# Low parts of weights by an adding DMA, and six more seven-product groups, in a hybrid decoder layer

## The chip, the cores and the metric

The kernel runs on one core of a Trainium2 chip. The metric is the device time of one launch in microseconds (us); lower is better. Times of several runs are given by their median.

## The reference

One decoder layer on a sequence of 256 tokens with 2048 features, all in float32: a norm and one combined projection, a state-space (SSD) head group and an attention head group, an output projection with a norm and residual, then a squared-ReLU MLP with a norm and residual. Cut to what matters here:

```python
def reference(x, ...):
    mix = hybrid_mixer(rmsnorm(h, norm_mix_pre), w_in, ..., w_out)   # w_in 2048 x 12320, w_out 4096 x 2048
    h = h + rmsnorm(mix, norm_mix_post)
    ff = squared_relu_mlp(rmsnorm(h, norm_mlp_pre), w_up, w_down)    # w_up 2048 x 8192, w_down 8192 x 2048
    return h + rmsnorm(ff, norm_mlp_post)

def squared_relu_mlp(u, w_up, w_down):
    hdn = jax.nn.relu(jnp.einsum('bsd,df->bsf', u, w_up))
    return jnp.einsum('bsf,fd->bsd', hdn * hdn, w_down)
```

Nearly all the work is the four matrix products of 256 tokens with these weights, each weight being used once.

## The kernel before, in words

**Split operands.** Products run on TensorE in a reduced float32 format. Every operand is therefore split into two parts: `hi`, a rounded copy, and `lo`, the rest (source minus hi). A product of two operands is three matmuls: hi by hi, hi by lo, lo by hi. ScalarE makes `hi` (L139, in `split`), VectorE makes `lo` by a subtraction (L140).

**Weight tiles.** A weight tile is 128 partitions by 2 row blocks by 512 columns (512 KB). `fetch` loads it from HBM on SP's queue into one of four `raw` buffers (L149; in w_out and in the last w_down the room `uc` serves as further raw buffers, through `fetch_next`). `parts` takes one of five `hi` and one of five `lo` buffers in turn. So tile number i can be split only when TensorE has done with tile number i - 5.

**Ordinary tiles.** `row_tile` (L262 to L264) multiplies one tile with one of the two token blocks: 2 row blocks by 3 matmuls, 128x512 each. An ordinary tile is thus 12 matmuls, and a row step k of a pair of column blocks (two tiles) 24.

**Seven-product groups.** `seven` replaces the pair of tiles of a row step by a fast scheme for 2 by 2 blocks, with seven block products instead of eight, so 21 matmuls (L344 to L346) instead of 24. In return VectorE makes four sums of weights (`add_in_line`, L225) and the sums, e, a and b, and a short t, are all split: four hi and four lo buffers a group. The sums of the activations of a row step are made once by `sums_of_acts` (L302 to L305 and a split) and kept, while their room lasts, for all column blocks. At the end of a pair of column blocks `combine_new` or `combine_onto` adds up what the groups left in further accumulators.

**Units.** `unit` does a pair of column blocks: a list of row steps (`order_of(steps, sevens)`), each ordinary or a group, then the last steps one column block at a time. The values of w_in, the whole of w_out, w_up and w_down run as units. w_up and w_down run in two halves of 4096 features (`hf`). The room for the sums is taken from tensors idle at that time: `in_place_of_u` (w_out and the last w_down: six sums), `in_place_of_h` (w_up three, the first w_down five).

**Order.** Loads, splits and additions of the units run ahead of TensorE: `high_priority` puts them first, and `in_line` keeps the splits and additions of VectorE and ScalarE in the order in which they are written. The scheduling layer fixes the order on each engine when the kernel is built; the engines then wait for one another by semaphores. `mw` holds the mixer's output and later that of w_down; `h` is kept in HBM meanwhile.

Of the kernel before, what the change touches and what calls it, by code (L numbers as in the profile page):

```python
# [10 lines left out]
F32 = mybir.dt.float32  # L11
F32R = mybir.dt.float32r
BF16 = mybir.dt.bfloat16
AF = mybir.ActivationFunctionType
ALU = mybir.AluOpType

P = 128
S = 256
D = 2048
NT = S // P  # L20
# [19 lines left out]
KB = 2  # L40
# [10 lines left out]
FIRST = 3  # L51
UP_SEVENS = (2, 4, 5)
V_SEVENS = (1, 3, 5, 6)


def constants():
# [18 lines left out]
def hymba_layer(ctx: ExitStack, tc: tile.TileContext, x, norm_mix_pre, w_in, conv_w, conv_b, dt_bias, a_log,  # L75
                d_skip, ssm_norm_w, w_out, norm_mix_post, norm_mlp_pre, w_up, w_down, norm_mlp_post,
                consts, out):
    nc = tc.nc
    w_in, w_out, w_up, w_down = w_in[0], w_out[0], w_up[0], w_down[0]
# [44 lines left out]
    def bank():  # L124
        return pacc.tile([P, NB], F32, name="acc")
# [10 lines left out]
    def split(hi, lo, src, scale=None):  # L136

        if scale is None:
            return (nc.scalar.activation(hi, src, AF.Copy),  # L139
                    nc.vector.tensor_tensor(lo, src, hi.bitcast(F32), op=ALU.subtract))  # L140
        return (nc.scalar.activation(hi, src, AF.Copy, scale=scale),  # L141
                nc.vector.scalar_tensor_tensor(lo, src, scale, hi.bitcast(F32), op0=ALU.mult, op1=ALU.subtract))

    def fetch(src, k0, c0, step=KB, into=None):

        raw = wp.tile([P, KB, NB], F32, name="raw", bufs=RAWS) if into is None else into
        for j in range(0, KB, step):
            rs = slice((k0 + j) * P, (k0 + j + step) * P)
            nc.sync.dma_start(raw[:, j:j + step], src[rs, c0:c0 + NB].rearrange("(k p) n -> p k n", p=P))  # L149
        return raw  # L150
# [13 lines left out]
    room = {}  # L164
# [6 lines left out]
        room["acts"] = part  # L171
        sums_of.clear()

    def in_place_of_h(acts):

        a = hp.tile([P, 3 * KB, 2, S], F32R, name="ha")
        room["sums"] = [a[:, k] for k in range(3 * KB)]
        if acts is part:
            b = hp.tile([P, KB, 2, S], F32R, name="hb")
            room["sums"] += [b[:, k] for k in range(KB)]  # L180
            room["sums"] += [hp.tile([P, 2, S], F32R, name="wpost", bufs=2) for _ in range(2)]
        else:
            b = hp.tile([P, NT, NB], F32, name="hb")
            room["shared"] = [[b[:, t] for t in range(NT)],
                              [hp.tile([P, NB], F32, name="wpost", bufs=2) for _ in range(NT)]]
        room["raw"] = None
        room["acts"] = acts
        sums_of.clear()
# [10 lines left out]
    def parts():  # L199
        return [wp.tile([P, KB, NB], F32R, name=n, bufs=BUFS) for n in ("hi", "lo")]  # L200
# [8 lines left out]
    line = {}  # L209

    @contextmanager
    def in_line():

        with ExitStack() as order:
            for last in line.values():
                order.enter_context(tc.issue_after(last.ins))
            yield

    def split_in_line(hi, lo, raw):
        with in_line():  # L220
            line["act"], line["dve"] = split(hi, lo, raw)

    def add_in_line(dst, a, b):
        with in_line():
            line["dve"] = nc.vector.tensor_tensor(dst, a, b, op=ALU.add)  # L225

    def weights(src, k0, c0, fetch=fetch):

        with tc.high_priority(offset=AHEAD):
            raw = fetch(src, k0, c0)  # L230
            hi, lo = parts()
            if fetch is fetch_next:
                split_in_line(hi, lo, raw)
                return hi, lo
            line.clear()
            with ExitStack() as order:
                while behind:
                    order.enter_context(tc.issue_after(behind.pop().ins))
                split(hi, lo, raw)
        return hi, lo  # L240
# [11 lines left out]
    def drain():  # L252
        while waiting:
            pump()
# [38 lines left out]
    def sums_of_acts(k):  # L293

        if k in sums_of:
            return sums_of[k]
        places = room["sums"][2 * len(sums_of):][:2]
        h_, l_, r = room["acts"](k * KB)
        with tc.high_priority(offset=AHEAD):
            a, c = (tmp().rearrange("p (i s) -> p i s", s=P) for _ in range(2))  # L300
            ah_, al_ = (v[:, r:r + KB].bitcast(F32).rearrange("p j (t s) -> p j t s", t=NT) for v in (h_, l_))
            nc.vector.tensor_tensor(a.rearrange("p (j t) s -> p j t s", t=NT), ah_, al_, op=ALU.add)  # L302
            nc.vector.tensor_tensor(c[:, 0:2], a[:, 0::3], a[:, 1:2].to_broadcast([P, 2, P]), op=ALU.subtract)
            nc.vector.tensor_tensor(c[:, 2], a[:, 0], c[:, 1], op=ALU.add)
            nc.vector.tensor_tensor(c[:, 3], a[:, 2], c[:, 2], op=ALU.subtract)  # L305
            ch, cl = (v.rearrange("p b (t s) -> p (b t) s", t=NT) for v in places)
            split(ch, cl, c)
        sums_of[k] = ch, cl
        return ch, cl
# [49 lines left out]
    def order_of(ks, by_seven):  # L359
        return [(k, k in by_seven) for k in ks]  # L360

    def unit(src, n, order, last, acc, more, combine, lag=0, at_end=(None, None), first=True, ending=None):


        cols = (n * NB, (n + 1) * NB)
        sevens = [k for k, by_seven in order if by_seven]
        for i, (k, by_seven) in enumerate(order):
            if i + 1 < len(order) and order[i + 1][1]:
                sums_of_acts(order[i + 1][0])
            if by_seven:  # L370
                if k == sevens[0]:
                    drain()
                seven(src, *cols, k, acc, more, k == sevens[0], k == sevens[-1])
            else:
                for b in range(2):
                    row_tiles(src, cols[b], [k], acc[b::2], room["acts"], first and i == 0, False,
                              fetch=fetch_next)
            if k == sevens[-1]:
                combine(more)
        for b in range(2):  # L380
            if b and ending:
                ended.append(ending(cols[b], last, acc))
            else:
                row_tiles(src, cols[b], last, acc[b::2], room["acts"], False, True, lag if b else 0, at_end[b],
                          fetch=fetch if b else fetch_next)
# [423 lines left out]
    def in_place_of_last_heads():  # L809
# [4 lines left out]
        yield  # L814
        for k in V_SEVENS:
            sums_of_acts(k)
            yield

    def two_values(vb):
# [8 lines left out]
        def end(b):  # L828
            def at_end(t, a):
# [5 lines left out]

        unit(w_in[:, COL_V:], vb, order_of(range(7), V_SEVENS), (7,), acc, more,
             lambda x: combine_new([[v[:, t] for t in range(NT)] for v in values], x), 0, (end(0), end(1)))
# [240 lines left out]
    acc = [bank() for _ in range(2 * NT)]  # L1078
    early = 5
# [7 lines left out]
    hp = ctx.enter_context(tc.tile_pool(name="hp", bufs=1, reuse_waits="tile"))  # L1087
# [11 lines left out]
    mw = hp.tile([P, NT, D], F32, name="mw")  # L1099
# [10 lines left out]
    more = [psmall(), bank(), psmall(), bank()]  # L1110

    def whole(n):
        def at_end(t, a):
# [1 line left out]
                mixed(n, t, a)  # L1115
        return at_end

    unit(w_out, 0, order_of(range(early, 14), (6, 9, 12)), (14, 15), acc, more,
         lambda x: combine_new(in_mw(0), x), 0, (whole(0), whole(1)), first=False)
    for n in (2, 3):  # L1120
        load_wpost(norm_mix_post, n)
    acc, more = more, acc
# [71 lines left out]
    def out_of_place():  # L1194

        yield from copies(in_dram, of_h, 4)
        in_place_of_h(act_u)
        for k in UP_SEVENS:
            sums_of_acts(k)
            yield  # L1200

    def in_dram(t, cs):
        return h_d[:, t, cs]
# [24 lines left out]
    acc = gemm_features(w_up, NB, begun)  # L1228
# [6 lines left out]
    acc, more = [bank() for _ in range(2 * NT)], [psmall(), bank(), psmall(), bank()]  # L1235
    for hf in range(2):
        if hf:
            in_place_of_h(act_u)
        for fb in range(0 if hf else 2, 8, 2):
            unit(w_up[:, hf * 4096:], fb, order_of(range(6), UP_SEVENS), (6, 7), acc, more,  # L1240
                 lambda x: combine_new(room["shared"], x), 0, (up_end(fb, 0), up_end(fb + 1, 1)))
            acc, more = more, acc
        if hf == 0:
            in_place_of_h(part)
            unit(w_down, 0, order_of(range(14), (4, 6, 9, 11, 13)), (14, 15), acc, more,
                 lambda x: combine_new(in_mw(0), x), 0, (onto(0), onto(1)))
            unit(w_down, 2, order_of((0, 1, 4, 2, 6, 3, 9, 5, 11, 7, 13, 8), (4, 6, 9, 11, 13)), (10, 12, 14, 15), more, acc,
                 lambda x: combine_new(in_mw(2), x), 0, (onto(2), onto(3)))
# [13 lines left out]
    in_place_of_u()  # L1262
    for n in range(2):
        load_wpost(norm_mlp_post, n)
    unit(w_down[4096:], 0, order_of(range(14), (3, 6, 8, 11, 13)), (14, 15), acc, more,
         lambda x: combine_onto(0, x), 0, (complete(0), complete(1)))
    for n in (2, 3):
        load_wpost(norm_mlp_post, n)
# [26 lines left out]
```

## Time and profile before

| | before |
|---|---|
| time, median of 3 runs | 1474.52 us (1473.16 to 1475.57) |
| profiled execution, first to last instruction | 1471.1 us |
| matmul records, TensorE busy | 7216, 1461.2 us (99%) |
| VectorE busy | 1239.6 us (84%) |
| ScalarE busy | 861.1 us (59%) |
| GpSimd busy | 47.8 us (3%) |
| read from HBM | 281.78 MB, 194 GB/s over the span |

The profiled execution has its span from the first to the last instruction; its own time is not listed apart from the three above, which lie 2.1 to 4.5 us over the span. Matmuls are pipelined and overlap one another, so the duration of one is longer than the step from one to the next. In the rows of the profile PE is TensorE, PEld its weight loads, DVE VectorE, ACT ScalarE, POOL GpSimd, SP the queue that issues the loads; L140 is line 140 of the kernel, and `lo<-raw,hi` names what an instruction writes and reads.

### The profile page before, as it was taken

How to read it: one execution, taken by the hardware profiler on the slowest of the kernel's cores; microseconds unless marked ns; L12 is line 12 of the kernel's file. 1: busy time of each engine (PE TensorE's matmuls, PEld its weight loads, DVE VectorE, ACT ScalarE, POOL GpSimd, SP SyncE). 2: the span in 40 equal slices, each digit the busy share in tenths (PEclk: the TensorE clock that was granted, in tenths of full speed). 3: DMA queues.
4: the chain of work that ended last, by engine and by line, in shares of the span. 5: the costliest groups of instructions: out<-in, count | busy, mean ns of one | idle time of the engine just before them, and what ended most of it. 6: DMA issues, size and time to landing. Idle time of an engine off the chain costs nothing.

```text
span 1471.1 us, 20006 instructions
## 1 busy us (share of the span) xinstructions
PE 1461.2 (99%) x7216; PEld 1231.4 (84%) x7216; DVE 1239.6 (84%) x1849; ACT 861.1 (59%) x1188; POOL 47.8 (3%) x67
## 2 busy tenths in 40 slices
PE   9999999999999999999999999999999999999998
PEld 8888888888888888888888888888888888888886
DVE  6798797898497696588989989889887898989998
ACT  7475675465456565555557566655554666665553
POOL 0003100210000000000000000000000000000000
PEclk9999999999999999999999999999999999999999
DMA  7665566555657476566657566655665666576853
GB/s 272 208 205 182 179 184 194 174 172 167 177 168 207 122 208 192 191 229 210 204 177 237 165 194 201 210 175 191 213 223 174 201 201 205 172 235 202 273 200 114
DMA packets 151299, 287.31 MB, mean 195 GB/s; under 512 B 11696, under 2 KB 14624, under 8 KB 151200
## 3 DMA queue, kind: packets, MB, share of 16 engines
q1 hardware_dynamic: 143472, 272.50, 58.9%
q10 hardware_dynamic: 7728, 13.54, 2.8%
q8 instruction: 56, 0.92, 0.3%
q14 instruction: 43, 0.35, 0.1%
HBM read 281.78 MB, written 4.23 MB: 194 GB/s over the span
## 4 chain that ended last, share of the span: by engine, by line
PE 94%; DVE 3%; issue 1%; ACT 1%; DMA 1%; POOL 0%; POOLq 0%; SPq 0%; ACTq 0%; DVEq 0%
PE acc L393 17%; PE acc L262 12%; PE acc L263 12%; PE acc L264 12%; PE acc L396 9%; PE acc L345 4%; PE acc L346 4%; PE acc L344 4%; PE ps L263 3%; PE ps L262 3%; PE ps L264 3%; PE ps L346 2%; PE ps L344 2%; PE ps L345 2%; DVE lo L140 1%
## 5 line engine op out<-in xcount | busy, mean ns | idle before, releaser
L139 ACT ACTIVATE hi<-raw 128x1024 fp32r<-128x1024 f32 (+1 forms) x477 | 499.0, 1053 | 387.9 <-PE acc L393 111.9
L140 DVE TENSOR_TENSOR lo<-raw,hi 128x1024 fp32r<-128x1024 f32 (+1 forms) x477 | 579.9, 1220 | 135.7 <-ACT hi L139 127.9
L393 PE MATMUL acc<-ua,hi 128*128 128x512 f32 x680 | 186.3, 402 | 0.0
L393 PEld LDWEIGHTS acc<-ua,hi 128*128 128x128 f32 x680 | 119.7, 189 | 18.7
L262 PE MATMUL acc<-hi,ua 128*128 128x512 f32 x280 | 112.0, 400 | 0.0
L396 PEld LDWEIGHTS acc<-ua,lo 128*128 128x128 f32 x680 | 99.8, 189 | 11.6
L264 PE MATMUL acc<-hi,ua 128*128 128x512 f32 x280 | 109.3, 391 | 0.0
L263 PE MATMUL acc<-lo,ua 128*128 128x512 f32 x280 | 109.3, 390 | 0.0
L396 PE MATMUL acc<-ua,lo 128*128 128x256 f32 x680 | 102.9, 281 | 0.0
L262 PE MATMUL acc<-hi,sh 128*128 128x512 f32 x224 | 88.7, 397 | 0.0
L264 PE MATMUL acc<-hi,sl 128*128 128x512 f32 x224 | 87.3, 390 | 0.0
L263 PE MATMUL acc<-lo,sh 128*128 128x512 f32 x224 | 87.3, 390 | 0.0
L139 ACT ACTIVATE hi<-e 128x1024 fp32r<-128x1024 f32 x51 | 54.1, 1062 | 55.5 <-DVE e L225 50.3
L393 PE MATMUL acc<-uc,hi 128*128 128x512 f32 x272 | 77.6, 398 | 0.0
L263 PE MATMUL acc<-lo,ah 128*128 128x512 f32 x168 | 65.5, 390 | 0.4 <-DVE lo L140 0.4
L264 PE MATMUL acc<-hi,al 128*128 128x512 f32 x168 | 65.4, 389 | 0.0
L262 PE MATMUL acc<-hi,ah 128*128 128x512 f32 x168 | 65.4, 389 | 0.0
L264 PEld LDWEIGHTS acc<-hi,ua 128*128 128x128 f32 x280 | 52.6, 188 | 11.6
L140 DVE TENSOR_TENSOR lo<-e,hi 128x1024 fp32r<-128x1024 f32 x51 | 62.0, 1216 | 0.0
L262 PEld LDWEIGHTS acc<-hi,ua 128*128 128x128 f32 x280 | 52.6, 188 | 10.4 <-ACT ua L141 0.3
L263 PEld LDWEIGHTS acc<-lo,ua 128*128 128x128 f32 x280 | 52.7, 188 | 10.0
L264 PE MATMUL acc<-hi,uc 128*128 128x512 f32 x144 | 56.0, 389 | 0.0
(475 smaller groups left out, 3060.9 us busy)
## 6 DMA issues: line engine op xcount, KB each, us to landing
raw<-in_w_in_dram SPq DMA_DIRECT2D x189, 512.0 KB, 3.6
raw<-in_w_up_dram SPq DMA_DIRECT2D x128, 512.0 KB, 3.9
raw<-in_w_down_dram SPq DMA_DIRECT2D x110, 512.0 KB, 4.7
raw<-in_w_out_dram SPq DMA_DIRECT2D x46, 512.0 KB, 4.2
uc<-in_w_out_dram SPq DMA_DIRECT2D x18, 512.0 KB, 4.5
uc<-in_w_down_dram SPq DMA_DIRECT2D x18, 512.0 KB, 5.1
bc<-acs_d ACTq DMA_DIRECT2D x8, 512.0 KB, 4.5
xs<-in_x_dram SPq DMA_DIRECT2D x8, 256.0 KB, 6.3
```

Source lines behind the costliest of these rows:

```text
L139: return (nc.scalar.activation(hi, src, AF.Copy), nc.vector.tensor_tensor(lo, src, hi.bitcast(F32), op=ALU.subtract))
L140: nc.vector.tensor_tensor(lo, src, hi.bitcast(F32), op=ALU.subtract))
L262: nc.tensor.matmul(dst, a_h[:, r, ts], hi[:, j], start=begin and j == 0, stop=False)
L263: nc.tensor.matmul(dst, a_h[:, r, ts], lo[:, j], start=False, stop=False)
L264: product[t] = nc.tensor.matmul(dst, a_l[:, r, ts], hi[:, j], start=False, stop=end and j == KB - 1)
L344: nc.tensor.matmul(dst, a_h, hi[:, j], start=own and first, stop=False)
L345: nc.tensor.matmul(dst, a_h, lo[:, j], start=False, stop=False)
L346: nc.tensor.matmul(dst, a_l, hi[:, j], start=False, stop=own and last)
L393: nc.tensor.matmul(acc[f], hi[:, j, f * P:(f + 1) * P], u(k0 + j), start=k0 + j == 0, stop=False, skip_group_check=True)
L396: nc.tensor.matmul(acc[f][:, 0], lo[:, j, f * P:(f + 1) * P], u(k0 + j)[:, 0], start=False, stop=k0 + j == NK - 1, skip_group_check=True)
```

## The change

It has two parts.

First, every third ordinary tile that is fetched through `fetch_next` (those of the units but for the last steps of a unit's second column block, and the first five row steps of w_out's first pair, which run ahead of its unit) gets its low part in another way. ScalarE writes the negated rounded copy into `lo`, then the rounded copy into `hi`; then a DMA issued from GpSimd's queue adds `raw` to `lo` in place. The sum is source minus hi, as before. VectorE has no part in these tiles; ScalarE makes two copies instead of one; `lo` and `raw` are in use until the DMA has landed.

Second, six row steps become seven-product groups: steps 8 and 10 in the first pair of column blocks of w_out (their activation sums were made for the second pair before; now they are made for the first and kept), step 1 in each of the three pairs of w_up's first half (its sum lies in the room of `mw`, which is taken anew before w_down), and step 9 in the first pair of the last w_down (its sum, too, was made for the second pair).

```diff
+BY_DMA = 3
...
-    def in_place_of_h(acts):
+    def in_place_of_h(acts, hf=0):
...
         room["sums"] = [a[:, k] for k in range(3 * KB)]
+        if acts is not part and not hf:
+            c = hp.tile([P, 4 * KB, 2, S], F32R, name="mw")
+            room["sums"] += [c[:, k] for k in range(4 * KB)]
...
+    turns = [0]
+
+    def split_by_dma(hi, lo, raw):
+
+        with in_line():
+            line["act"] = nc.scalar.activation(lo, raw, AF.Copy, scale=-1.0)
+        with in_line():
+            line["act"] = nc.scalar.activation(hi, raw, AF.Copy)
+        nc.gpsimd.dma_start(lo.bitcast(F32), raw, accum_op=ALU.add)
...
             if fetch is fetch_next:
-                split_in_line(hi, lo, raw)
+                turns[0] += 1
+                if turns[0] % BY_DMA:
+                    split_in_line(hi, lo, raw)
+                else:
+                    split_by_dma(hi, lo, raw)
                 return hi, lo
...
-    unit(w_out, 0, order_of(range(early, 14), (6, 9, 12)), (14, 15), acc, more,
+    unit(w_out, 0, order_of(range(early, 14), (6, 8, 9, 10, 12)), (14, 15), acc, more,
...
             sums_of_acts(k)
             yield
+        sums_of_acts(1)
...
         if hf:
-            in_place_of_h(act_u)
+            in_place_of_h(act_u, hf)
         for fb in range(0 if hf else 2, 8, 2):
-            unit(w_up[:, hf * 4096:], fb, order_of(range(6), UP_SEVENS), (6, 7), acc, more,
+            unit(w_up[:, hf * 4096:], fb, order_of(range(6), UP_SEVENS if hf else (1,) + UP_SEVENS), (6, 7), acc, more,
...
             in_place_of_h(part)
+            mw = hp.tile([P, NT, D], F32, name="mw")
...
-    unit(w_down[4096:], 0, order_of(range(14), (3, 6, 8, 11, 13)), (14, 15), acc, more,
+    unit(w_down[4096:], 0, order_of(range(14), (3, 6, 8, 9, 11, 13)), (14, 15), acc, more,
```

## The prediction

> **What bounds the kernel now.** I read the page's busy table and its chain first, then the waits of TensorE, then the groups by shape, and last the order of time around one seven-product group.
>
> ```profile
> span 1471.1 us, 20006 instructions
> PE 1461.2 (99%) x7216; PEld 1231.4 (84%) x7216; DVE 1239.6 (84%) x1849; ACT 861.1 (59%) x1188; POOL 47.8 (3%) x67
> PE acc L263 <- DVE lo L140: 0.4, 1, 0.4
> PE acc L345 <- DVE lo L140: 0.3, 1, 0.3
> ```
>
> TensorE is busy for 1461.2 of 1471.1 us, and the low parts that VectorE makes (L140) held a matmul up only twice, for 0.4 and 0.3 us. So the end is set by the number of matmuls, as long as weights are ready. VectorE has 84%, ScalarE 59%. The span is one execution; the three times of the kernel are 1473.16 to 1475.57, median 1474.52, that is 3.4 us above the span. I carry these 3.4 us unchanged and add differences to 1474.5.
>
> How nearly the weights come too late is in the order of time behind a seven-product group of w_up (833.60 to 838.36):
>
> ```profile
> 833.14 0.39 PE L263 MATMUL acc<-lo,ua 128*128 128x512 f32 x1
> 833.37 0.39 PE L264 MATMUL acc<-hi,ua 128*128 128x512 f32 x1
> 833.60 0.39 PE L344 MATMUL ps<-hi,ua 128*128 128x512 f32 x1
> 838.36 0.39 PE L262 MATMUL acc<-hi,ua 128*128 128x512 f32 x1
> 838.58 0.39 PE L263 MATMUL acc<-lo,ua 128*128 128x512 f32 x1
> 833.80 1.06 ACT L139 ACTIVATE hi<-raw 128x1024 fp32r<-128x1024 f32 x1 [2.09 <-PE acc L264]
> 834.89 2.59 DVE L140 TENSOR_TENSOR lo<-raw,hi 128x1024 fp32r<-128x1024 f32 x2 [2.46 <-ACT hi L139]
> ```
>
> Columns are start, duration, engine, line, operation. Matmuls start every 0.227 us (833.60 to 838.36 is one group, 21 matmuls, 4.76 us); the 0.39 us overlap. There are five hi and five lo buffers, and a group takes four of each. So the first ordinary tile behind a group can only be split when TensorE has left the ordinary tile ahead of the group: its last lo product starts at 833.14, ScalarE starts at 833.80 (released by L264), VectorE's two subtractions run from 834.89, the first done after about 1.2 us, and TensorE wants the lo at 838.58. About 2.4 us are to spare. That margin is what this change spends.
>
> **The matmuls that go.** An ordinary pair of tiles is 24 matmuls, a group 21. Six pairs become groups: 18 matmuls of 0.227 us, 4.1 us off the path. Their weight loads and the transfers from HBM stay the same in number. This is the whole gain that TensorE can show: 0.28%.
>
> **What VectorE and ScalarE get and lose.**
>
> ```profile
> L140 DVE TENSOR_TENSOR lo<-raw,hi 128x1024 fp32r<-128x1024 f32 x471 | 575.8, 1227 | 135.5 <-ACT hi L139 127.9
> L139 ACT ACTIVATE hi<-raw 128x1024 fp32r<-128x1024 f32 x471 | 495.3, 1058 | 387.9 <-PE acc L393 111.9 <-PE acc L264 85.9 <-issue 51.9
> L140 DVE TENSOR_TENSOR lo<-r,hi 128x512 fp32r<-128x512 f32 x51 | 34.9, 683 | 2.7 <-ACT hi L139 2.7
> L139 ACT ACTIVATE hi<-r 128x512 fp32r<-128x512 f32 x51 | 31.6, 619 | 9.9 <-PE ps L264 5.2 <-PE acc L264 4.7
> L225 DVE TENSOR_TENSOR raw<-raw 128x512 f32<-128x512 f32 x54 | 36.8, 682 | 0.0
> ```
>
> The changed instruction order holds 57 adding transfers on GpSimd's queue. VectorE loses 57 subtractions of 1.23 us, 70 us; ScalarE gains 57 negated copies of 1.06 us, 60 us, which its 59% hides in the mean. A group costs VectorE four additions of 0.68, three subtractions of 1.23 and a short one of 0.68, 7.1 us, where a pair costs 2.5: six times 4.6 is 28 us more. ScalarE's 1.06 + 0.62 more per group make 10 us. None of this is on the path in the mean. In places it is, below.
>
> **When the adding transfer lands.** ScalarE must first write the negated copy, then GpSimd issues, then the transfer reads two operands and writes one. In the stretch shown: the lo buffer is free at 833.14 + 0.39 = 833.5, the copy is done 1.06 later, at 834.6, and with 0.1 us for each of two hand-overs (an estimate from 833.80 + 1.06 = 834.86 to VectorE's 834.89, rounded up for two engines) TensorE, which wants the lo at 838.58, is held up by all of the transfer above 3.75 us. No transfer of this kind is in the trace. The nearest rows:
>
> ```profile
> raw<-in_w_in_dram SPq DMA_DIRECT2D x189, 512.0 KB, 3.6
> raw<-in_w_down_dram SPq DMA_DIRECT2D x110, 512.0 KB, 4.7
> out_dram<-ha SPq DMA_DIRECT2D x2, 256.0 KB, 2.3
> ha<-h_d ACTq DMA_DIRECT2D x6, 256.0 KB, 6.9
> q1 hardware_dynamic: 143472, 272.50, 58.9%
> ```
>
> The last columns are the median us to landing; in the queue's row, MB and share of the 16 engines' span. 512 KB once take 3.6 us in a quiet stage and 4.7 in a busy one. q1 moved 272.5 MB in 58.9% of 1471 us, so 512 KB (0.524 MB) fill all engines for 1.67 us. A second read that adds this gives 3.6 + 1.67 = 5.3 us, which I take. The ends: 2.3 us (a write half as large, with the second read free) and 7 us (the slowest row).
>
> The Trainium skill, "DMA: Bandwidth & Descriptors", section on the anatomy of one DMA on the gpsimd path, gives about 2.0 us plus bytes over 436 GB/s, so an estimate of 3.2 us here; its page "Collectives: The Full Stack", section Why ReduceScatter is half of AllGather, says that a reducing transfer is slower for its two reads and not for its addition, which makes 4.4. By 4.4 the term below would be 6 instead of 20; no run shows yet which holds.
>
> **What that costs.** In the changed order I counted for each of the 57 tiles the matmuls between its lo buffer's last use and its own first lo product, at 0.227 us. Thirteen stand right behind a group: 23 matmuls, 5.2 us, in nine of them, 5.4 to 6.1 where transposes lie between. Eighteen stand one tile later: 29 matmuls, 6.6 us, in thirteen, 6.8 to 7.3 in five. Four have 7.9 to 8.2, and 22 in ordinary stretches 11.3 to 12.6. Against each stand 1.47 us (5.22 - 3.75) plus the transfer. At 5.3 us that is 6.77: 9 x 1.55 + 3.5 for the other four of the first kind, 13 x 0.19 of the second, in all 20 us. At 3.75 it is 0, at 4.4 it is 6, at 6 it is 41, at 7 it is 73. TensorE has no spare time in which to win it back.
>
> **Where VectorE runs over.**
>
> ```profile
> 632.00:676.00 44.00, 44.00 (x196) 36.43 (x195) 40.32 (x54) 26.51 (x29) 0.00 (x0) 1.00 0.77 257
> 853.54:897.00 43.46, 43.46 (x200) 35.91 (x199) 38.66 (x47) 28.36 (x35) 0.00 (x0) 1.00 0.64 194
> 1316.09:1357.57 41.48, 41.48 (x185) 34.35 (x183) 39.15 (x52) 22.87 (x25) 0.00 (x0) 1.00 0.64 209
> 632.48 1.22 DVE L140 TENSOR_TENSOR lo<-raw,hi 128x1024 fp32r<-128x1024 f32 x1
> 636.23 0.39 PE L345 MATMUL ps<-lo,sh 128*128 128x512 f32 x1
> 650.24 0.68 DVE L302 TENSOR_TENSOR r<-ah,al 128x512 f32<-128x512 f32 x1
> 654.13 0.42 DVE L303 TENSOR_TENSOR r<-r 128x256 f32<-128x256 f32 x1
> 655.60 0.28 DVE L304 TENSOR_TENSOR r<-r 128x128 f32<-128x128 f32 x1
> 656.93 0.28 DVE L305 TENSOR_TENSOR r<-r 128x128 f32<-128x128 f32 x1
> ```
>
> The columns of the first three are the stretch, its length, then busy time of PE, PEld, DVE, ACT. In w_out's first pair of blocks (first row) VectorE is busy for 40.3 of 44 us, and it starts this stretch with little lead: the group's first lo is done at 633.7 for 636.23, 2.5 us. Two groups more cost 9.2 us there, and two activation sums (0.68 + 0.42 + 0.28 + 0.28 and the short subtraction, 2.3 each) another 4.7, because the sums for 8 and 10 move here from the next pair of blocks; two of the ordinary tiles by transfer give back 2.4. That is 51.8 us of VectorE against 44 - 1.4 = 42.6 of TensorE: 9.2 over, less the lead of 2.5, 6.7. From 9.2 it may fall to 3.5, as 14 of a group's 21 matmuls need only hi (3.2 us of work to put ahead). I take 5.5. It is not free elsewhere: w_out's second pair loses two sums, but TensorE does not wait there.
>
> In w_up's first half, VectorE's 38.7 of 43.5 become 38.7 + 4.6 - 2.4 = 40.9 against 42.8, which fits, with the one new sum hidden; in w_down's last first pair 39.2 + 4.6 + 2.3 - 2.4 = 43.7 against 40.8, 2.9 over, which the lead of the ordinary tiles ahead covers (0 to 3, I take 0). The reallocation of mw waits for groups long done: 0, as their matmuls stand first in each unit. GpSimd's queue carries nothing behind a transfer but the six single-column powers of the norms, whose transfers ahead are all long landed: 0. On SP's queue the load that reuses a raw buffer waits until the transfer has read it, about 1.06 + 5.3 against 1.06 + 1.2, 4 us later; the raws of ordinary stretches are needed as they land, but TensorE has a lead there. I take 0, and up to 10 in all.
>
> Sum: 1474.5 - 4.1 + 20 + 5.5 = 1496 us.
>
> **The rivals.** First, *the transfer is in time*: it takes 3.75 us or less since the second read overlaps the first, so that the 3.6 us row holds. VectorE is then relieved at no cost; if also the w_out overrun is filled with hi products, only the 18 matmuls remain: 1470.4, faster. For it: the 3.6 us row and 22 tiles with much more room. Against: that row is one read in a quiet stage, and a second read and the loads beside it (58.9% of the engines) can only add to it. The skill's 3.2 us is this case. Second, *in time, but VectorE's overrun in w_out eats the gain*: 1474.5 - 4.1 + 5.5 = 1476, no change that can be told. Third, *the transfer takes 7 us*, as the slow row of 256 KB does: 73 us of waits and some 5 from raws held long, 1474.5 - 4.1 + 73 + 5.5 + 5 = 1554. A page rule lies on this side: the skill's "SBUF — State Buffer", section Who interferes with whom, has descriptors that GpSimd writes starve under VectorE's two-port modes, but not under additions and subtractions of two tensors; no row here can show it. That the change would not do what it says is excluded for its parts by the instruction order (57 transfers, 18 matmuls fewer).
>
> **How the numbers follow.** The forecast of transfers between 4.2 and 6.5 us gets 0.68 (1480 to 1532), the first rival 0.13, the second 0.09, the third 0.10. A measurement tells 0.2%, about 3 us, from no change: faster is the first rival, 0.13; same is the second, 0.09; slower the rest, 0.78. The range leaves out the third and a part of the first rival: 1472 to 1535, its upper end is a transfer of 6.5 us with the overrun (1532) and 3 us for raws.
>
> **What would show it.** Right: lo products of ordinary tiles that wait for the DMA of their lo, up to 31 of them, 0.2 to 1.6 us each, at the first or second tile behind a group; landing near 5.3 us; a hold in w_out near 640 to 665 ended by VectorE; VectorE near 1200 us, TensorE's matmuls 18 fewer. Wrong: landings under 4 us and no wait for them, or waits in the ordinary stretches too, which would mean that raw buffers or the load of the DMA engines decide.

## The result, and the profile after

The changed kernel takes 1615.4 us (median of four runs, 1601.7 to 1620.1) against 1474.1 us before: the ratio is 1.094 (95% interval 1.090 to 1.099), 141 us more. The forecast was 1496 us, in a range to 1535: the direction was right, and the size far too small.

The busy table of the changed kernel:

```profile
span 1611.1 us, 20206 instructions
PE 1502.2 (93%) x7198; PEld 1242.3 (77%) x7198; DVE 1209.4 (75%) x1833; ACT 917.7 (57%) x1258; POOL 97.2 (6%) x124
```

The span grew by 140.0 us. TensorE lost 18 matmuls, as meant, but is busy for 41.0 us longer (1502.2 against 1461.2), and idle for 108.9 us of the span instead of 9.9, 99.0 more. So two things have to be explained: new idle time, and matmuls that became slower. The waits of TensorE in the changed kernel (us in all, how often, the longest) tell the first:

```profile
PE acc L281 <- DMA lo<-raw: 47.9, 22, 4.2
PE ps L281 <- DMA lo<-raw: 26.0, 13, 4.1
PE acc L362 <- ACT hi L140: 8.8, 12, 1.1
PE acc L281 <- DMA lo<-uc: 6.6, 5, 1.8
PE ps L281 <- DMA lo<-uc: 3.1, 2, 1.9
PE ps L281 <- DVE lo L141: 2.0, 3, 0.8
```

L281 is the lo product of an ordinary tile (L263 before). The four DMA rows are 83.6 us: 42 waits for a low part that the adding transfer has not brought yet. By the tile's place they are 26 us at the 13 tiles right behind a group, 41 us at the 18 one tile later, 7 at the four with 7.9 to 8.2 us of lead, and 9 at seven of the 22 in ordinary stretches. (The lead is the work that TensorE has between the last use of the tile's lo buffer and the tile's own first lo product.) The DMA issues, and the queues' rows:

```profile
raw<-in_w_up_dram SPq DMA_DIRECT2D x128, 512.0 KB, 4.2
lo<-raw POOLq DMA_DIRECT2D x49, 512.0 KB, 6.6
lo<-uc POOLq DMA_DIRECT2D x8, 512.0 KB, 6.7
q1 hardware_dynamic: 143472, 272.50, 55.3%
q0 software_dynamic: 8208, 29.89, 9.8%
```

An adding transfer lands 6.6 us after its issue in the median (the 57 lie between 4.4 and 9.9); at the 13 tiles right behind a group the median is 5.6, at the 18 one tile later 6.8. One of them in the order of time, the first tile behind a group of w_down (the group's 21 matmuls lie between the first and the fourth row):

```profile
1117.89 0.39 PE L281 MATMUL acc<-lo,sh 128*128 128x512 f32 x1
1118.32 1.06 ACT L232 ACTIVATE lo<-raw 128x1024 fp32r<-128x1024 f32 x1 [0.24 <-PE acc L281]
1119.67 0.86 POOL L235 DMA_DIRECT2D lo<-raw  x1 [15.32 <-DVE lo L141]
1123.11 0.39 PE L280 MATMUL acc<-hi,sh 128*128 128x512 f32 x1
1125.25 0.50 PE L281 MATMUL acc<-lo,sh 128*128 128x512 f32 x1 [1.75 <-DMA lo<-raw]
```

The buffer's last reader ends at 1118.28, ScalarE's negated copy runs to 1119.38, GpSimd issues 0.29 us later, and TensorE, out of work at 1123.50, starts again at 1125.25, 5.6 us after the issue.

The slower matmuls stand in the order of time behind a longer wait, at 871 us, with two windows (the stretch, its length, busy us of PE, PEld, DVE, ACT, POOL, then the granted clock, the DMA share and GB/s):

```profile
868.00:871.78 3.78, 0.91 (x4) 0.78 (x5) 3.66 (x6) 1.79 (x3) 0.00 (x0) 1.00 0.37 110
871.78:875.19 3.41, 3.41 (x10) 2.63 (x9) 1.19 (x3) 0.35 (x1) 0.00 (x0) 0.50 0.92 290
870.87 0.50 PE L281 MATMUL acc<-lo,ua 128*128 128x512 f32 x1 [3.71 <-DMA lo<-raw]
873.27 0.63 PE L280 MATMUL acc<-hi,ua 128*128 128x512 f32 x1
873.70 0.63 PE L281 MATMUL acc<-lo,ua 128*128 128x512 f32 x1
875.55 0.39 PE L363 MATMUL acc<-lo,ua 128*128 128x512 f32 x1
875.78 0.40 PE L364 MATMUL acc<-hi,ua 128*128 128x512 f32 x1
```

After 3.71 us without work the granted clock is 0.50 for 3.41 us: matmuls start every 0.43 us instead of 0.227. There are 14 such stretches, 3.4 us long early and 6.8 us later, the last of them at the very end, where the kernel before has one too. They all start on one grid of 3.413 us. Thirteen of the 14 follow a window of that grid in which TensorE stood idle for 62% or more (the other one 43%), and no window at full clock that is without a stretch behind it was idle for more than 55%. So what counts is not the length of one wait but the idle share of a grid window. A stretch lasts a second window where the first was idle again for 24% or more; in the seven of one window it was 4% at most. The traces of all 14 kernels together show the same: of the 92 half-clock stretches whose window before lies inside TensorE's work, 90 follow a window with 52% or more of idle time (the others 43 and 47%), and none of the 6071 full-clock windows without a stretch behind them was idle for more than 57%. The cores view shows the sum, before and after:

```profile
core 0: 1471.1 us, clock 0.998
core 0: 1611.1 us, clock 0.978
```

A mean of 0.978 is 2 x 0.022 x 1611 = 71 us at half clock, against 6 us before. VectorE (1209.4 us) and the 7198 matmuls are as forecast.

### The profile page after: what moved, and what is told of

It is laid out like the page before. It is cut to its first block, busy times and chain, and to the rows that moved or that the text cites. A ratio compares the mean times of both kernels' runs of the same rounds, so it can differ in the third digit from the quotient of the medians.

```text
span 1611.1 us, 20206 instructions
## 1 busy us (share of the span) xinstructions
PE 1502.2 (93%) x7198; PEld 1242.3 (77%) x7198; DVE 1209.4 (75%) x1833; ACT 917.7 (57%) x1258; POOL 97.2 (6%) x124
## 5 line engine op out<-in xcount | busy, mean ns | idle before, releaser
L140 ACT ACTIVATE hi<-raw 128x1024 fp32r<-128x1024 f32 (+1 forms) x428 | 446.9, 1050 | 393.5 <-PE acc L411 101.4
L141 DVE TENSOR_TENSOR lo<-raw,hi 128x1024 fp32r<-128x1024 f32 (+1 forms) x428 | 522.0, 1222 | 195.6 <-ACT hi L140 189.3
L281 PE MATMUL acc<-lo,ua 128*128 128x512 f32 x260 | 105.8, 407 | 20.1 <-DMA lo<-raw 20.0
L281 PE MATMUL acc<-lo,sh 128*128 128x512 f32 x224 | 90.9, 406 | 22.3 <-DMA lo<-raw 16.2
L280 PE MATMUL acc<-hi,ua 128*128 128x512 f32 x260 | 104.9, 406 | 0.0
L282 PE MATMUL acc<-hi,ua 128*128 128x512 f32 x260 | 104.6, 402 | 0.0
L235 POOL DMA_DIRECT2D lo<-raw x49 | 42.4, 865 | 994.2 <-ACT lo L232 800.1
L281 PEld LDWEIGHTS acc<-lo,ua 128*128 128x128 f32 x260 | 50.4, 194 | 33.8 <-DMA lo<-raw 24.1
L281 PEld LDWEIGHTS acc<-lo,sh 128*128 128x128 f32 x224 | 43.5, 194 | 36.2 <-DMA lo<-raw 19.9
L239 DVE TENSOR_TENSOR e<-raw 128x512 f32<-128x512 f32 x51 | 35.1, 689 | 47.3 <-DMA raw<-in_w_up_dram 22.7
L141 DVE TENSOR_TENSOR lo<-e,hi 128x1024 fp32r<-128x1024 f32 x57 | 69.5, 1220 | 0.0
L281 PE MATMUL acc<-lo,ah 128*128 128x512 f32 x148 | 59.1, 399 | 9.3 <-DMA lo<-raw 8.7
L232 ACT ACTIVATE lo<-raw 128x1024 fp32r<-128x1024 f32 x49 | 51.6, 1054 | 24.6 <-DMA raw<-in_w_up_dram 7.0
L281 PE MATMUL acc<-lo,uc 128*128 128x512 f32 x144 | 57.4, 399 | 3.0 <-DMA lo<-raw 3.0
```

Source lines behind the costliest of these rows:

```text
L140: return (nc.scalar.activation(hi, src, AF.Copy), nc.vector.tensor_tensor(lo, src, hi.bitcast(F32), op=ALU.subtract))
L232: line["act"] = nc.scalar.activation(lo, raw, AF.Copy, scale=-1.0)
L235: nc.gpsimd.dma_start(lo.bitcast(F32), raw, accum_op=ALU.add)
L280: nc.tensor.matmul(dst, a_h[:, r, ts], hi[:, j], start=begin and j == 0, stop=False)
L281: nc.tensor.matmul(dst, a_h[:, r, ts], lo[:, j], start=False, stop=False)
L282: product[t] = nc.tensor.matmul(dst, a_l[:, r, ts], hi[:, j], start=False, stop=end and j == KB - 1)
```

## The experiments

In all of them GpSimd, ScalarE and VectorE do as in the changed kernel unless the edit says otherwise, and "idle" is the span less TensorE's busy time (9.9 us before, 108.9 after), "half clock" 2 x (1 - mean clock) x span.

**The two parts apart.** The first kernel keeps the six groups and makes every low part on VectorE, the second has before's groups and keeps the transfers (61, since the count of every third tile falls differently).

```diff
# groups only
-                if turns[0] % BY_DMA:
+                if True:
# transfers only
-    unit(w_out, 0, order_of(range(early, 14), (6, 8, 9, 10, 12)), ...
+    unit(w_out, 0, order_of(range(early, 14), (6, 9, 12)), ...
...
```

> The six groups without any adding transfer; every low part by VectorE. If the changed kernel's loss is all from the transfers (late landings, and the slower TensorE clock that goes with the waits), this stands near the kernel before: 1470 us if VectorE's additional work in w_out is hidden, 1476 if its overrun of about 5.5 us shows, as the prediction had it. Rival, the groups cost much by themselves because VectorE becomes the bound: above 1490 us, with lo products that wait for VectorE.

> The transfers without the six groups. If the loss is the transfers': about 1615 to 1620 us, with some 80 us of waits for the DMA of lo and a granted clock near 0.98. Rival, groups and transfers harm each other (less lead behind more groups): 1560 us or less.

The groups alone: 1492.3 us, 1.012 (1.011 to 1.014), 18 us slower with 18 matmuls fewer, the size that the rival gave. The transfers alone: 1581.3 us, 1.073 (1.070 to 1.076), 107 us, between the two values that were expected. Together they cost 141, some 16 more than the sum. That groups shorten the leads that the transfers need would explain this rest; it is argued, and small beside the 18 us between the four times of the changed kernel. For the groups, the windows of w_out's first pair and of w_up's first half, and the largest wait of TensorE:

```profile
632.00:676.00 44.00, 37.61 (x161) 29.22 (x159) 43.79 (x66) 23.12 (x28) 0.00 (x0) 1.00 0.59 203
755.00:940.00 185.00, 176.61 (x826) 142.22 (x825) 166.48 (x245) 116.25 (x180) 3.56 (x4) 1.00 0.58 180
PE acc L362 <- ACT hi L140: 14.3, 16, 1.8
```

and the second window before:

```profile
755.00:940.00 185.00, 183.84 (x873) 152.23 (x872) 162.46 (x235) 118.17 (x180) 3.56 (x4) 1.00 0.63 193
```

In w_out VectorE is busy for 43.8 of 44 us and TensorE loses 6.4 us against its 44.00 before, where 5.5 had been forecast. In w_up it loses 7.2 us where nothing had been forecast, although VectorE is at only 90% (166.5 of 185). (The page of this kernel is at 1490.4 us of span and 1465.5 us of TensorE.) The two account for 13.6 of the 15.0 us by which the idle time grew (24.9 against 9.9). The wait goes through ScalarE's `hi`: the first matmul of a group (L362) wants the hi of a sum that VectorE makes, ScalarE then splits and VectorE subtracts from, all in one fixed order on both engines. What VectorE itself waited for during w_up's three pairs of this run (840 to 955 us, VectorE busy for 93%) is mostly weight loads:

```profile
DVE e L239 <- DMA raw<-in_w_up_dram: 6.2, 5, 1.7
DVE lo L141 <- ACT hi L140: 0.7, 2, 0.3
```

In the kernel before it had no such wait for a load there. The changed kernel, where transfers relieve VectorE, shows the same hold in w_up's first half (834 to 1010 us): VectorE is at 79% there, and groups still wait for their hi:

```profile
834.00:1010.00 176.00, 155.58 (x684) 123.99 (x683) 138.98 (x181) 107.85 (x137) 6.91 (x8) 0.97 0.64 179
PE acc L362 <- ACT hi L140: 6.8, 9, 1.1
```

So it is the chain from a load over VectorE's sum to ScalarE's hi that comes late, while VectorE's busy sum leaves room. Which link sets it is not shown.

**The price of the addition.** The same transfer without adding (lo then holds the plain source; TensorE runs the same matmuls on it, and the true low part is left out of the result):

```diff
-        nc.gpsimd.dma_start(lo.bitcast(F32), raw, accum_op=ALU.add)
+        nc.gpsimd.dma_start(lo.bitcast(F32), raw)
```

> The changed kernel with the 57 transfers as plain copies (raw to lo, no addition, so one read instead of two; lo then holds raw, and the low part is left out of the computation). Theory: the second read costs about 1.1 us of engine time (2.8 us of all engines per adding transfer against 1.7 for a load of the same size), so the landing falls from 6.6 to about 5.5 us, the waits from 84 to some 35 us and the clock's loss with them: 1535 to 1560 us. Rival, the landing is issue and latency under load and not the addition: landing stays above 6.2 us, time above 1595 us.

1549.1 us, 1.051 (1.047 to 1.056). Its issue and queue rows:

```profile
lo<-raw POOLq DMA_DIRECT2D x49, 512.0 KB, 5.5
q0 software_dynamic: 8208, 29.89, 4.9%
```

The same packets and bytes take half the share of the engines: a packet of 4096 bytes 0.159 us, and 0.328 us where it is added. The landing falls only from 6.6 to 5.5 us, the waits for lo from 83.6 to 35.5, the half clock from 71 to 18 us. So the addition costs 1.1 us a tile and, through waits and clock, 66 of the 141 us. The larger part of a landing is not the data's: by an estimate from these rows, 128 packets spread evenly over 16 engines are 8 each, 2.6 us of the 6.6 with the addition and 1.3 of the 5.5 without.

**Half the bytes.** Row block 0 of such a tile is subtracted by VectorE, only block 1 goes by transfer:

```diff
-            line["act"] = nc.scalar.activation(lo, raw, AF.Copy, scale=-1.0)
+            line["act"] = nc.scalar.activation(lo[:, 1], raw[:, 1], AF.Copy, scale=-1.0)
...
-        nc.gpsimd.dma_start(lo.bitcast(F32), raw, accum_op=ALU.add)
+            line["dve"] = nc.vector.tensor_tensor(lo[:, 0], raw[:, 0], hi[:, 0].bitcast(F32), op=ALU.subtract)
+        nc.gpsimd.dma_start(lo[:, 1].bitcast(F32), raw[:, 1], accum_op=ALU.add)
```

> The changed kernel with only the second row block (j = 1) of the 57 tiles by an adding transfer of 256 KB; the first by VectorE. TensorE needs the second row block 0.7 us after the first, and the transfer should land about 0.9 us earlier (half of 1.7 us of engine time). Theory of the lead: 1.6 us less wait at each of some 43 waiting tiles, 84 to about 25 us, and the clock's loss mostly gone: 1520 to 1545 us. Rival, the landing does not shorten with the size: waits fall by 0.7 us each only, to 55 us, 1565 to 1590 us.

1543.0 us, 1.047 (1.045 to 1.049), as expected.

```profile
lo<-raw POOLq DMA_DIRECT2D x49, 256.0 KB, 5.4
```

Half of the data lands 1.2 us earlier, and the kernel is 72 us faster than the changed one: the waits for lo fall to 27.6 us. The first packet of an adding transfer starts 1.4 us after the issue at best, and 2.0 in the median of the changed kernel. That the rest of a landing is queueing beside the loads is argued from this, not shown.

**The clock.** Eight matmuls of zeros stand ahead of the first lo product of those 35 transferred tiles that have a group among the four tiles ahead, so that TensorE works while it waits; 280 matmuls more in all.

```diff
+            for _ in range(FILL if id(lo) in late else 0):
+                nc.tensor.matmul(dst[:120], zero, hi[:, j], start=False, stop=False)
```

> The changed kernel with eight more matmuls (a zero tile times hi, into the same accumulator, 1.8 us in all) ahead of the first lo product of each of the 35 transferred tiles that have a group among the four tiles before them; the sum is unchanged. Those tiles wait 1.2 to 4.2 us in the changed kernel. Theory: the half clock of TensorE in 14 stretches comes from its idle time and costs some 40 us beside the waits; with the waits filled the clock stays near 1.0 and the time falls to 1575 to 1590 us although there is more work. Rival, the lower clock has another cause, or costs little: 1615 to 1640 us, with the same half-clock stretches.

```profile
span 1597.5 us, 20775 instructions
PE 1545.4 (97%) x7478; PEld 1283.7 (80%) x7478; DVE 1208.7 (76%) x1834; ACT 918.5 (57%) x1258; POOL 97.2 (6%) x124
core 0: 1597.5 us, clock 0.991
```

1599.4 us, 1.085 (1.083 to 1.087): 16 us faster than the changed kernel with 280 matmuls more (7478 records instead of 7198). The half clock falls from 71 to 29 us. The books agree: 280 x 0.227 = 63.6 us of work were added, TensorE's busy time grew by 43.2, so 20.4 us went elsewhere. Counted from one matmul's start to the next, the matmuls in half-clock stretches took 26 us more than at full clock in the changed kernel and 11 us more here, 15 fewer; and there are 27 breaks in TensorE's work fewer (40 over 0.15 us instead of 67), each worth some 0.16 us, 4 us together. So the idle time lowers the clock, and the 65 us of half clock that the change brought cost about 27 us of time (TensorE had work for 55 of the 65). The four executions of the changed kernel go the same way: granted clock 0.984, 0.978, 0.974 and 0.972 with spans of 1599.9, 1611.1, 1616.1 and 1618.3 us. The forecast that the time would fall to 1575 to 1590 was too good: 29 us of half clock are left, waits for lo too (34 us instead of 83.6), and some 7 us of the fillers did not fall into idle time (63.6 less the 56.8 by which it shrank).

**Only far tiles.** A counter keeps the transfers to tiles with four ordinary tiles ahead: first with the six groups, then with before's.

```diff
+            since[0] += 1
-                if turns[0] % BY_DMA:
+                if turns[0] % BY_DMA or since[0] < 5:
...
+        since[0] = 0
```

> Transfers only for the 22 of the 57 tiles that have four ordinary tiles ahead of them (a lead of 11.3 us and more), the six groups kept. Theory of the lead: a transfer of 6.6 us with 1.8 us ahead of it fits in 11.3, so nearly all waits go: 1472 to 1485 us, clock 1.0. Rival, the transfers cost by their load on the DMA engines and by the raw buffers that they hold, wherever they stand: about 22/57 of the loss, 1525 us.

> Transfers only for those 22 tiles that have four ordinary tiles ahead of them, and none of the six groups: the kernel before with nothing but far transfers. Theory of the lead: with 11.3 us and more of lead, a landing of 6.6 us costs TensorE nothing, so 1474 to 1480 us, and the remaining loss of the far-only kernel (46 us) is the groups' 18 and what the groups' thin margins add. Rival, a transfer costs by what it holds or by load wherever it stands (28 us for 22): 1495 to 1505 us.

With the groups (22 transfers): 1519.9 us, 1.031 (1.029 to 1.033); the largest wait of TensorE is that of groups only again (a group's first matmul, L365 here, waits 14.4 us for ScalarE's hi), and the waits for lo are 10.8. With before's groups (23 transfers): 1493.2 us, 1.014 (1.011 to 1.016).

```profile
lo<-raw POOLq DMA_DIRECT2D x21, 512.0 KB, 6.9
PE acc L283 <- DMA lo<-raw: 4.5, 4, 2.0
SPq L150 <- DMA lo<-raw: 128.8, 21, 9.2
```

Both are slower than the theory of the lead, which held far transfers to be free, and near the rival. TensorE waits for a far lo for only 4.9 us, yet the kernel is 19 us slower, with waits of about 5 us for low parts by VectorE and 2 for ScalarE's hi. The last row shows a candidate: the queue of the loads stood 21 times for 6 us on the mean, because the raw buffer that it wants is still read by an adding transfer.

**Raw freed earlier.** The transfer reads `hi` instead of `raw` (the sum is then zero, so the low part is left out); raw is free after ScalarE's two copies. First in the changed kernel, then with far tiles and before's groups. The transfer also starts one copy (1.04 us) later than before, so each of these runs changes two things.

```diff
-        nc.gpsimd.dma_start(lo.bitcast(F32), raw, accum_op=ALU.add)
+        nc.gpsimd.dma_start(lo.bitcast(F32), hi.bitcast(F32), accum_op=ALU.add)
```

> The changed kernel with the transfer's source taken from hi instead of raw (the low part becomes zero and is left out of the computation): raw is free after ScalarE's two copies, as hi is held anyway. But the transfer can only be issued when hi is there, 1.06 us later. Theory that raw buffers held by the transfer delay the next loads and with them the start of later tiles (SP waits 276 us for the transfers): starts after the release go back to 0.4 us, waits at tiles of ordinary stretches vanish; at the tiles behind groups they grow by 1.06 us each; together 1600 to 1640 us with SP's waits for lo gone. Rival, raw buffers do not matter: plus 31 x 1.06 = 33 us and some clock, above 1650 us.

> The far transfers without the groups (22 tiles, plus 20 us as measured), but the source taken from hi instead of raw (the low part of these 22 tiles becomes zero and is left out). Raw buffers are free after ScalarE's copies; the transfer starts 1.06 us later, which a lead of 11.3 us covers. Theory that the held raw buffer is the price of a far transfer (the next load waits for the landing): most of the 20 us go, 1474 to 1481 us. Rival, the price is the load on the DMA engines or ScalarE's second copy in the line: 1488 to 1500 us.

The changed kernel becomes 1738.5 us, 1.180 (1.178 to 1.182), with these waits and landing:

```profile
PE acc L281 <- DMA lo<-hi: 108.7, 26, 6.4
PE ps L281 <- DMA lo<-hi: 59.1, 14, 6.3
lo<-hi POOLq DMA_DIRECT2D x57, 512.0 KB, 8.1
```

The far tiles alone become 1505.2 us, 1.023 (1.021 to 1.024), with

```profile
lo<-hi POOLq DMA_DIRECT2D x23, 512.0 KB, 8.2
PE acc L283 <- DMA lo<-hi: 15.1, 6, 4.1
```

In the changed kernel the queue of the loads had this wait:

```profile
SPq L150 <- DMA lo<-raw: 276.5, 49, 10.7
```

In both runs it is gone: the loads no longer stand behind a transfer, and with far tiles the waits for ScalarE and VectorE of the run before are gone as well. But more other transfers, nearly all of them loads, overlap with an adding transfer (4.6 instead of 2.6 on the mean in the changed kernel, 5.4 instead of 3.2 with far tiles), and it lands after 8.1 instead of 6.6 us, 8.2 instead of 6.9. So the theory that the held raw buffers set the time does not hold: both kernels became slower without the hold, by 123 and 12 us. The likely reason is that the hold was throttling the loads, and that the transfers profited. That the longer landing comes from the loads is argued from these two pairs, not shown by a run that changes the loads alone.

**The groups spread.** No transfers, groups of w_up's first half and w_down alone, w_up's steps in another order (0, 1, 3, 2, 6, 4, 5, 7), to put an ordinary step between group 1 and 2.

```diff
-            unit(w_up[:, hf * 4096:], fb, order_of(range(6), UP_SEVENS if hf else (1,) + UP_SEVENS), (6, 7), acc, more,
+            unit(w_up[:, hf * 4096:], fb, order_of(range(6), UP_SEVENS) if hf else order_of((0, 1, 3, 2, 6, 4, 5), (1,) + UP_SEVENS),
+                 (6, 7) if hf else (7,), acc, more,
```

> No transfers; four of the six groups (w_up's first half, w_down), and in w_up's first half the order of the row steps changed to 0, 1, 3, 2, 6, 4, 5, 7 so that an ordinary step stands behind each of the first two groups. If w_up's 10 us in the groups-only kernel come from pairs of adjacent groups, spreading them saves most: 1471 to 1476 us, at best 2.7 us under the kernel before (12 matmuls of 0.227 us). Rival, VectorE's sum over the unit decides (38.7 + 4.6 = 43.3 us against TensorE's 42.8) whatever the order: 1480 to 1486 us.

1484.5 us, 1.008 (1.007 to 1.010). TensorE's busy time in the window of w_up is 177.64 us, so 6.2 us are still lost there instead of 7.2: that the first two groups stand next to each other is not the cause. (Groups 4 and 5 stay adjacent, as in the kernel before.)

**GpSimd subtracts.** No second copy and no transfer; GpSimd makes the 57 low parts itself.

```diff
-            line["act"] = nc.scalar.activation(lo, raw, AF.Copy, scale=-1.0)
...
-        nc.gpsimd.dma_start(lo.bitcast(F32), raw, accum_op=ALU.add)
+        nc.gpsimd.tensor_tensor(lo, raw, hi.bitcast(F32), op=ALU.subtract)
```

> The same 57 low parts by a subtraction on GpSimd instead of the negated copy and the transfer, the six groups kept. From GpSimd's 0.68 to 0.73 us for 128x256, 128x1024 should take about 2.5 us, so a tile is ready 3.7 us after its release, within the lead of 5.2 us. Theory that only the lateness of the transfer hurts: no waits for lo, VectorE relieved by 70 us, so better than the groups alone: 1470 to 1485 us. Rival, VectorE and GpSimd hold each other up when both read two tensors from SBUF: VectorE's subtractions get longer where GpSimd runs, 1490 to 1530 us.

1527.8 us, 1.037 (1.035 to 1.038). Groups by shape:

```profile
L233 POOL TENSOR_TENSOR lo<-raw,hi 128x1024 fp32r<-128x1024 f32 x49 | 132.9, 2713 | 839.2 <-ACT hi L232 745.1 <-PE ps L804 68.2 <-DVE lo L141 18.3
L237 DVE TENSOR_TENSOR e<-raw 128x512 f32<-128x512 f32 x51 | 43.8, 858 | 31.1 <-DMA raw<-in_w_up_dram 15.7 <-DMA raw<-in_w_down_dram 13.4 <-PE ps L810 2.0
```

GpSimd needs 2.71 us where VectorE needs 1.22, and holds VectorE up meanwhile: its additions of two raw halves take 858 ns instead of 689, single subtractions up to 3.3 us, and with 57 subtractions fewer it is busy as long as with groups only (1266.6 us against 1267.7). The Trainium skill, "SBUF — State Buffer", section Who interferes with whom, has this: a VectorE instruction with two SBUF inputs contends with a GpSimd instruction that reads SBUF. The rows agree. It is 88 us faster than the changed kernel all the same, but 36 slower than groups only.

**The second copy alone.** Before's groups; ScalarE writes the negated copy as well, and VectorE still makes every low part.

```diff
-            line["act"] = nc.scalar.activation(hi, raw, AF.Copy)
-        nc.gpsimd.dma_start(lo.bitcast(F32), raw, accum_op=ALU.add)
+            line["act"], line["dve"] = split(hi, lo, raw)
```

> The kernel before with ScalarE's negated copy at all 57 tiles, but no transfer: VectorE then writes lo as it always did. Same result as before. If the second copy is hidden by ScalarE's 59% (the assumption of the prediction): 1473 to 1476 us. Rival, in the line each copy of 1.06 us delays hi and so VectorE: at the margins of 2.4 us behind groups it is still hidden, but where VectorE runs behind it is not, 1480 to 1500 us.

1476.0 us, 1.002 (1.001 to 1.003): 61 copies more on ScalarE cost 2 to 4 us in all. No version here was faster than the kernel before.

## Why the prediction was wrong, point by point

**The 18 matmuls.** 7198 records instead of 7216, as forecast. Their 4.1 us can't be seen beside the rest.

**The transfer's landing: this step failed, in its size.** The mechanism was right: all 31 tiles within two places of a group wait, at the first and second tile behind a group. The size was off by a factor of four, 20 us forecast and 83.6 measured, for two reasons. The landing was taken as 3.6 (the row of a quiet stage) plus 1.67 us, 5.3; it is 6.6. The row of the busy stage, 4.7, which the prediction had quoted beside it, gives 6.4 with the same second read, and the weights that matter are loaded in busy stages. The prediction's own formula gives 59 us at 6.6. The other 25 us come from later starts and from spread. After the end of the buffer's last lo product the negated copy begins 0.04 us later in the median right behind a group, but 0.6 us later in the median one tile on, and 2.5 to 3.3 us later at six of those 18: ScalarE is then busy with the split tiles that stand ahead in its line, or waiting for a sum of VectorE. And with landings from 4.4 to 9.9 every late one costs while an early one gains nothing. Right behind a group, where the landing was 5.6 in the median, 17.5 us were forecast and 26 came; the second tile behind a group, forecast at 2.5 us for all 18, cost 41. A step of leads so close together (5.2, 6.6, 7 us) had to be taken with a spread, not at one value. Of the two figures that the prediction took from the Trainium skill, the 3.2 us by the fit of "DMA: Bandwidth & Descriptors" (section on the anatomy of one DMA on the gpsimd path) lies below the least of the 57, and the 4.4 with the two reads of "Collectives: The Full Stack" is that least one; the measured median is 6.6.

**What the waits do to the clock: this step was missing.** The prediction counted a matmul at 0.227 us throughout. The 65 us at half clock cost about 27 us, by the matmuls' steps, and the filler run bears it out. The kernel before shows granted clock 1.00 everywhere but at its very end, so nothing in its profile stood for this. Waits of 0.2 to 1.6 us, as forecast, would mostly have stayed below the idle share that lowers the clock (some 55% of a window of 3.41 us, 1.9 us); many of those of 2 us and more did not. The Trainium skill, "TensorE: Matmul & The Clock Gate", Part 1 and the section HAM oscillation — how this bites in real kernels, has TensorE fall to half rate after an idle window of about 3.4 us, also when waits for a DMA return again and again. The trace agrees on the unit (stretches of 3.41 and 6.83 us), but less idle time was enough: one stretch follows a single wait of 2.4 us, another three waits of 1.05, 0.22 and 1.21. A further 10 us is the tail of the last matmul ahead of each break, since the trace has 71 breaks in TensorE's work instead of 7, and each shows a matmul's 0.39 us instead of its 0.227 step. Together: 99 us idle, and -4 + 27 + 10 of the 41 us of busy time. Some 8 us stay open: matmuls at full clock whose steps are slightly longer than before.

**VectorE's overrun in w_out: right.** 5.5 us forecast, 6.4 in the run with groups only. The forecast counted 2.4 us of relief by transfers, which that run does not have, so the mechanism is borne out and the close number is in part luck. In the changed kernel 3.0 us of such waits, for ScalarE's hi, are left in this stretch beside 5.0 for transfers, so adding the whole 5.5 was too much.

**"w_up's first half fits": this failed.** VectorE's 40.9 of 42.8 us was read as room. 7.2 us are lost in the run with groups only, and in the changed kernel the groups there wait 6.8 us for their hi with VectorE at 79%: a busy sum that fits says nothing of a chain that runs from a load over VectorE to ScalarE. Together with w_out's 6.4 us that is most of what turns the groups alone from a gain of 4 us into a loss of 18.

**ScalarE's second copy hidden: right** within 2 to 4 us. **Raw buffers held longer at 0, up to 10: wrong in kind.** Holding them costs the loads time (276.5 us of SP's waits) and gains it for the transfers; 23 far transfers cost 19 us with hardly a wait for them. How much of that is the hold and how much the load of the DMA engines stays open: freeing the buffer changed both.

**The rivals.** The third, a transfer of 7 us (1554 us), was the nearest: the landing was 6.6, its 73 us of waits the right order of size, and it lacked the clock. The first two, in time, were out by the landing alone. Of its signs for being wrong, waits in ordinary stretches came (9 us at seven tiles), and they did point to the raw buffers and the load of the DMA engines: at four of the seven the negated copy had itself waited for the tile's load, and the seven landings are 6.7 to 9.9 us.

## What to carry to other kernels

Handing work from a busy engine to a transfer needs a lead longer than the slowest landing in the stage where it runs, not the median in a quiet one; count it from the copy's real start, and compare with the lead of each tile. When TensorE has had no idle time, price a new wait at more than its length: here about 99 us of idle time brought some 37 us of slower and interrupted matmuls, and waits that fill over half of a 3.41 us window are the ones that cost the clock. Where a chain runs from loads through two engines, a busy share of 80 or 90% is no proof of room.

## What was not expected of the hardware

A packet of 4096 bytes takes 0.328 us where it is added and 0.159 where it is copied, so a reducing transfer occupies the engines twice as long; yet its landing is only 1.1 us longer. Halving the bytes takes 1.2 us off 6.6. GpSimd is busy for 0.86 us to issue an adding transfer, 0.54 for a plain one. Half clock came after waits as short as 2.4 us: it follows the idle share of fixed windows of 3.413 us, with the turn between 43 and 57%.
